# Scratch stores and loads of a two-layer hybrid backbone, issued from GpSimd and ScalarE instead of SyncE

## The chip, the cores and the metric

The kernel runs on one core of a Trainium2 chip. The metric is the device time of one execution in microseconds; the median of three runs is given with the lowest and the highest. The profile is of one execution, and times inside it count from the start of its span. Engines are named as in the profile: PE is TensorE (its weight loads are PEld), DVE is VectorE, ACT is ScalarE, POOL is GpSimd, SP is SyncE. A name with a q behind it (SPq, POOLq) is the engine's instruction queue, where DMAs are issued and waits stand.

## The reference

Two layers work on 512 latent and 256 context tokens of width 1024 in float32. Each layer normalises and modulates its tokens and multiplies them with one wide input matrix. Its columns feed four mixers: A, attention over all tokens with normalised queries and keys and a rotary step; B, a gating unit that mixes positions inside blocks of 128; C, attention in a window of 128 tokens with a sink; D, an mLSTM that scans six blocks in both directions. What joins them is this:

```python
def merge_branches(ys, p, w_br, w_o):
    gates = (p['a_gate'], p['w_gate'], p['g_gate'], p['m_gate'])
    y = jnp.stack([yk * jax.nn.silu(gk) for yk, gk in zip(ys, gates)], axis=2)
    proj = jnp.einsum('bnkw,kwd->bnkd', y, w_br)
    m = p['merge']
    g = jax.nn.sigmoid(m.reshape(m.shape[0], m.shape[1], N_BRANCH, D_MODEL))
    return jnp.sum(g * proj, axis=2) @ w_o
```

The result is normalised, gated and added to the tokens. In the second layer the outputs of context tokens are not needed.

## The kernel before

Tokens lie in tiles of 128: latent tiles 0 to 3 and context tiles 4 and 5. Each matrix product is made of three passes with the high and low parts of both factors, in a 32-bit format that PE takes (fp32r). A weight block goes through `emit_load` (L210): two DMAs into staging buffers `wr` (three of them, L222), ScalarE makes the high part `wh` (L224), VectorE the low part `wl` (L225); there are two buffers of each.

A layer has two stages. In the **mixer stage** two threads are interleaved at the time the program is built (`interleave`, L1219). The dense thread multiplies the tokens with column blocks of the input matrix, in an order chosen from `FILL_ORDER` (L71), and each block has its own ending: gates (`gate_unit`, L545), the sigmoids of the merge that are computed early (`early_unit`, L559), the mLSTM's output gate (`mo_unit`, L573) and its convolved q, k and v (`m_unit`, L586). Until they are needed these results lie in **scratch tensors** in device memory: `sgd`, `thd`, `omd`, `zd`. The mixer thread runs attention A, the mLSTM's gate arithmetic (`gate_math`, L854), window attention, and the four heads of the mLSTM (`mlstm_prep`, L947, and `mlstm_scan`, L1007). It reads the mLSTM's inputs back (L957, L1019), reads rows of `nmd` spread over all partitions (L987; ScalarE's L991 is the first to use them) and stores the branches' outputs to `ydram` (L837, L1068) and the softmax sums to `rsd` (L831). The gating unit (`spatial`, L619) runs in the merge stage of layer 0 and in the mixer stage of layer 1; it stores through `turn_out` (L673).

In the **merge stage** (`merge`, L1266) the four branches follow each other. For each of four column tiles the branch's output `yt` and gate `sg` are read back (L1279, L1280), for the two attentions also the inverted sums `rs`, each row spread over 64 partitions (two DMAs, L1284). VectorE multiplies them (L1286, L1287), ScalarE and VectorE split the product into `gh` and `gl` (L1288, L1289), and PE multiplies those with the branch's projection for eight column tiles; an early sigmoid `th` is read back for each (L1300). `yt`, `sg`, `rs` and `th` come from one pool of eight buffers `m`. `finish` (L1357) makes the output projection, normalises and adds; in layer 0 it stores the new tokens (L1412) and prepares the next layer's input.

`rstd` (L352) computes a power of -1/2 on GpSimd (L354): 72 small instructions, GpSimd's only work besides four fills at the start.

Every DMA but two at the start (ScalarE, L152 and L163) is issued from the SyncE queue, in order. The framework orders each engine's instructions by priority in a simulated time line and adds the waits; the order on hardware is then fixed, engine by engine. An instruction whose data or buffer is not ready holds everything behind it on its engine.

Of the kernel before, what the change touches and what calls it, by code (L numbers as in the profile page):

```python
# [83 lines left out]
def tile_hybrid_block(ctx, tc, A, out):  # L84
# [61 lines left out]
    # constants  # L146
# [131 lines left out]
    def side(units):  # L278
        """Units of later uses, their rows of weights summed up by VectorE, in small steps."""
        def load(l, i, half):  # L280
            raw = wp.tile([128, UW // 2], F32, tag="wr", name="wr", bufs=3)[:, :1024]
            sy.dma_start(out=raw, in_=A["w_mod"][l, i][:, half * 1024:half * 1024 + 1024])
            return v3(raw, 4)

        sums = None
        for l, i in units:
            ns = 2 if l == 0 or i < 8 else 1
            for half in range(2):
                raw = load(l, i, half)
                yield  # L290
                if half == 0:
                    if sums is not None:
                        side_sums(*sums)
                    acc = [T1() for _ in range(ns)]
                    sums = (l, i, acc)
                for k in range(4):
                    kk = 4 * half + k
                    for s in range(ns):
                        if kk == 0:
                            dve.tensor_scalar(acc[s], raw[:, k, :], cH[:, kk, s:s + 1], None, op0=ALU.mult)  # L300
                        else:
                            dve.scalar_tensor_tensor(out=acc[s], in0=raw[:, k, :], scalar=cH[:, kk, s:s + 1],
                                                     in1=acc[s], op0=ALU.mult, op1=ALU.add)
                    if k % SIDE_K == SIDE_K - 1 and k < 3:
                        yield
        yield
        side_sums(*sums)
# [36 lines left out]
    def load_gates(l, i):  # L344
        if i % 2 == 0:
            g = gate_g[l, i // 2] = M(512)
            sy.dma_start(out=g, in_=bc(gates[l][0:1, i * 256:i * 256 + 512], [128, 512]))
        if l == 0:
            gate_c[i] = XS()
            sy.dma_start(out=gate_c[i], in_=bc(gates[l][1:2, i * 256:i * 256 + 256], [128, 256]))  # L350
# [73 lines left out]
    def seg_mm(wh, wl, mh, ml, nk, seg):  # L424
        """One column tile over one token segment."""
        ps = DB()
        n = seg.stop - seg.start
        for k in range(nk):
            mm(ps[:, :n], wh(k), mh(k)[:, seg], k == 0, False)
            mm(ps[:, :n], wh(k), ml(k)[:, seg], False, False)  # L430
            mm(ps[:, :n], wl(k), mh(k)[:, seg], False, k == nk - 1)
        return ps[:, :n]
# [16 lines left out]
    def rope_tables(g):  # L449
        """cos and sin rows times a norm's weights; sin by its source half."""  # L450
        tab = M(512).rearrange("p (s t d) -> p s t d", s=2, t=XT)
        gv = bc(g.rearrange("p (o d) -> p o d", o=1), [128, XT, 64])
        dve.tensor_mul(tab[:, 0], cosT, gv)
        dve.tensor_mul(tab[:, 1], sinT, gv)
        return tab[:, 0], tab[:, 1]

    def evacuate(ps, nh, g):
        """First stage of a tile of heads: out of PSUM, with the norm's factors."""
        n = nh * 64
        e, a = T1()[:, :n], T1()[:, :n]  # L460
        act.copy(e, ps[:, :n])
        r = None
        if g is not None:
            act.activation(a, ps[:, :n], AF.Square)
            ss = YD(4)[:, :nh]
            dve.tensor_reduce(out=ss, in_=a.rearrange("p (h d) -> p h d", h=nh), op=ALU.add, axis=AX.X)
            r = rstd(YD(4)[:, :nh], ss, nh, 64.0, EPS)
        return e, a, r

    def rotate(ear, nh, t, g, tabs, copies):  # L470
        """Second stage: norm, rotary and the split into copies of high and low parts."""
        e, a, r = ear
        shape = [128, nh, 64]
        ev, av = (z.rearrange("p (h d) -> p h d", h=nh) for z in (e, a))
        if r is not None:
            dve.tensor_mul(ev, ev, bc(r.rearrange("p (h o) -> p h o", o=1), shape))
        if t < XT:
            dve.tensor_mul(av, ev, bc(tabs[0][:, t:t + 1, :], shape))
            dve.tensor_mul(ev, ev, bc(tabs[1][:, t:t + 1, :], shape))
            dve.tensor_add(av[:, :, 0:32], av[:, :, 0:32], ev[:, :, 32:64])  # L480
            dve.tensor_add(av[:, :, 32:64], av[:, :, 32:64], ev[:, :, 0:32])
            ev, e = av, a
        elif g is not None:
            dve.tensor_mul(ev, ev, bc(g.rearrange("p (o d) -> p o d", o=1), shape))
        st = ST()
        sv = st.rearrange("p (h s d) -> p h s d", h=nh, s=2 * copies)
        f = e.rearrange("p (h o d) -> p h o d", h=nh, o=1).to_broadcast([128, nh, copies, 64])
        act.copy(sv[:, :, 0:copies, :].bitcast(F32R), f)
        dve.tensor_sub(sv[:, :, copies:, :].bitcast(F32R), f, sv[:, :, 0:copies, :])
        return st  # L490
# [11 lines left out]
    def drain(n2, n3):  # L502
        """Runs the waiting stages of earlier tiles, all but the last n2 and n3."""
# [41 lines left out]
    def gate_unit(l, b, i, sgd, segs):  # L545
        w = in_unit(l, f"gate{b}_{i}")
        for c in range(2):
            for seg in segs:
# [7 lines left out]
                sy.dma_start(out=sgd[b, 2 * i + c][:, seg], in_=th[:, :n])  # L556
                yield seg_us(seg)

    def early_unit(l, name, thd, segs):  # L559
        b, i = int(name[1]), int(name[3])  # L560
        wh, wl = take(("in", l, name))
        for c in range(2):
            mh, ml = (v3(w[:, c * 1024:c * 1024 + 1024], 8) for w in (wh, wl))
            for seg in segs:
# [5 lines left out]
                sy.dma_start(out=thd[b, 2 * i + c][:, seg], in_=th[:, :n])  # L570
                yield seg_us(seg)

    def mo_unit(l, i, omd, nq):  # L573
# [3 lines left out]
        for t in range(nq):  # L577
# [5 lines left out]
            sy.dma_start(out=omd[2 * i:2 * i + 2, :, t * 128:(t + 1) * 128].rearrange("h p d -> p h d"), in_=v3(th, 2))  # L583
            yield TOK_US

    def m_unit(l, i, zd, res):  # L586
        taps = res["taps"]
        w = in_unit(l, f"m{i}")
        for c in range(2):
# [3 lines left out]
            for seg in segs:  # L593
# [11 lines left out]
                sy.dma_start(out=zd[j][:, seg], in_=zz)  # L605
# [4 lines left out]
    def gelu2(dst, ps, acc=None):  # L610
        """dst = 2 gelu(ps), and its sum over the columns"""
# [61 lines left out]
    def turn_out(v, dst):  # L673
# [5 lines left out]
        sy.dma_start(out=dst.rearrange("g p t -> p g t"), in_=v3(ys, 2))  # L679
# [22 lines left out]
    def attend_scores(qT, kv, kT, hl, pair, mode, sc, sink, sums):  # L702
        is_x = pair[0] < XT
        Ps = []
        for t in pair:
            ps = S()
            qs = qT[:, hl, t * 128:(t + 1) * 128]
            # pieces: (psum column, key column, count)
# [44 lines left out]
    def attend_values(Ps, Vt, kv, pair, mode, yT, hl):  # L753
        is_x = pair[0] < XT
        # blocks: (key tile, first query, number of queries)
# [41 lines left out]
    def attention(l, mode, b, ydram, rsd, res):  # L797
# [26 lines left out]
        # the queries' sums, inverted and as rows, to divide by where the branch is read back  # L824
# [6 lines left out]
        sy.dma_start(out=rsd[b].rearrange("h (t q) -> (h t) q", q=128), in_=rows[:8 * nq, :])  # L831

    def finish_attend(pend, ydram, b, mode):
        Ps, Vt, kv, pair, yT, hl, hp = pend
        yield from attend_values(Ps, Vt, kv, pair, mode, yT, hl)
        if hl % 2 == 1:
            sy.dma_start(out=ydram[b, 2 * kv + hp][:, pair[0] * 128:pair[0] * 128 + 256], in_=yT)  # L837

# [15 lines left out]
    def gate_math(l, G):  # L854
        """All decay quantities, laid out as (direction, chunk, head) columns."""
# [63 lines left out]
        # floor: 2 exp(-(b + max(m_prev, cummax u)))  # L919
# [16 lines left out]
        # rows of -M_t  # L936
# [6 lines left out]
        sy.dma_start(out=nmd, in_=oth)  # L943
# [3 lines left out]
    def mlstm_prep(h, gm, zd, nq, res):  # L947
# [7 lines left out]
        for r, z in enumerate((qT, kT, vT)):  # L955
            n = nq * 128 if r == 0 else NTOK
            sy.dma_start(out=z[:, :n], in_=zd[3 * h + r][:, :n])  # L957
        # token-layout k and v
# [12 lines left out]
        # S^T, shared by the directions  # L971
# [12 lines left out]
        for d in range(2):  # L984
            rows = gm["nmd"][d * 32 + h:d * 32 + h + 24:4, :][:nq]
            nm, qs, kw = B2[:, 2 * d, :], B2[:, 2 * d + 1, :], (vT, kT)[d]
            sy.dma_start(out=v3(nm[:, :n], nq),  # L987
# [19 lines left out]
    def mlstm_scan(l, h, gm, pre, omd, nq, ydram):  # L1007
# [4 lines left out]
        for s in range(NT):  # L1012
# [4 lines left out]
            if s == NT - 2:  # L1017
                om = M(768)
                sy.dma_start(out=om[:, :n], in_=omd[h][:, :n])  # L1019
# [32 lines left out]
        # per-head norm, output gate, transposition  # L1052
# [15 lines left out]
        sy.dma_start(out=ydram[3, h][:, :n], in_=H[:, :n])  # L1068
        yield 0.7

# [54 lines left out]
    def needs(name):  # L1125
        """Buffers of the two pools that a unit takes."""
        return int(name[:2] == "w_" or name == "g_v0"), int(name in ("w_kv", "g_v0"))

    def pick(left, cur, res):
        """The first unit left that needs not wait once the current one has its buffers."""  # L1130
# [74 lines left out]
    def fits(res, c):  # L1205
        """Whether a mark is set, or a pool has so many free buffers."""
# [12 lines left out]
    def interleave(X, Dn, res, ratio):  # L1219
        """Emits the mixers' steps and the dense steps in proportion; each may wait for marks of the other."""  # L1220
# [4 lines left out]
        def dstep():  # L1225
            """Cost of one dense step, or None when it has to wait or has ended."""
# [39 lines left out]
    def merge(l, ydram, rsd, sgd, thd):  # L1266
# [8 lines left out]
        for bi, b in enumerate(BRANCHES):  # L1275
            gh, gl = BIG([128, 4, NTOK], F32R), BIG([128, 4, NTOK], F32R)
            for k in range(4):
                yt, sg = M(768), M(768)
                sy.dma_start(out=yt[:, :n], in_=ydram[b, k][:, :n])  # L1279
                sy.dma_start(out=sg[:, :n], in_=sgd[b, k][:, :n])  # L1280
                if b < 2:
                    rs = M(768)
                    for i in range(2):
                        sy.dma_start(out=rs[64 * i:64 * i + 64, :n],  # L1284
# [5 lines left out]
            for j in range(KT):  # L1290
# [5 lines left out]
                if (l, b, j // 2) in EARLY:  # L1296
# [3 lines left out]
                    sy.dma_start(out=th[:, :n], in_=thd[b, j][:, :n])  # L1300
# [92 lines left out]
    def finish_tile(l, t, o, sst, xdram):  # L1393
# [17 lines left out]
        if t < XT:  # L1411
            sy.dma_start(out=xdram[t], in_=o)  # L1412
# [11 lines left out]
    def next_x(t, xn):  # L1424
        """Normalised and modulated input of the next layer, transposed and split."""
# [48 lines left out]
def _layout(I):  # L1474
# [46 lines left out]
    # shape constants  # L1521
# [39 lines left out]
```

## Time and profile before

| | |
|---|---|
| Runs, us | 2069.32, 2072.67, 2073.26; median 2072.67 |
| Profiled execution, span, us | 2072.0 |
| PE busy | 2006.9 us (97%), 13196 matmuls |
| PEld, DVE, ACT, POOL busy | 88%, 64%, 47%, 3% |
| DMA | 274.97 MB, mean 133 GB/s, q1 40.5% of the 16 engines' time |

The profiled execution is known by its span; the page gives no other time for it. PE's busy time is nearly the whole span in every slice but the first and the last ones. A busy PE means that matmuls are under way; they overlap, so it does not say how close to its peak PE is. A row of waits tells who stood idle, for whom, how long in all, how often, and the longest single wait. Waits of an engine that is not the bottleneck cost nothing by themselves.

### The profile page before, as it was taken

The page shows a single profiled execution, that of the slowest core. Times are in us where ns is not written, and L with a number is a line of the kernel's source. Part 1 is how long each engine was busy: PE and PEld are TensorE (multiplying, and loading weights), DVE is VectorE, ACT ScalarE, POOL GpSimd, SP SyncE. Part 2 cuts the span into 40 slices and gives each one's busy share as a digit, 9 for nine tenths or more (in the row PEclk, how much of TensorE's full clock was granted, in tenths as well). Part 3 has the DMA queues.
Part 4 walks back from the last instruction along what each step waited for, and adds up shares of the span by engine and source line. Part 5 has one row for each costly group of instructions (what it writes and reads, how often), then busy time and mean ns, then how long its engine had stood idle before and what let it go on. Part 6 is the DMA issues. An engine that isn't in the chain of part 4 may idle for free. (4 is left out here: it accounts for less than half of the span.)

```text
span 2072.0 us, 34558 instructions
## 1 busy us (share of the span) xinstructions
PE 2006.9 (97%) x13196; PEld 1816.9 (88%) x13196; DVE 1321.5 (64%) x2861; ACT 978.5 (47%) x2195; POOL 69.0 (3%) x76
## 2 busy tenths in 40 slices
PE   7999999999999999999999999999999999999998
PEld 4998998999999898889998999989989898887777
DVE  5766766676556665648545588667676575555765
ACT  6565554344444444324432376655554465433333
POOL 0200100000000000001000022000000000000000
PEclk9999999999999999999999999999999999999999
DMA  7212223323333534665334352223334325447745
GB/s 279 73 44 85 81 86 115 123 98 112 122 117 96 172 122 149 198 206 184 114 116 140 123 190 67 86 96 112 92 121 139 123 90 161 147 147 224 246 136 178
DMA packets 133142, 274.97 MB, mean 133 GB/s; under 512 B 16176, under 2 KB 52208, under 8 KB 132592
## 3 DMA queue, kind: packets, MB, share of 16 engines
q1 hardware_dynamic: 132688, 272.69, 40.5%
q8 instruction: 104, 1.70, 0.3%
q14 instruction: 62, 0.51, 0.1%
q10 hardware_dynamic: 288, 0.07, 0.0%
HBM read 219.33 MB, written 53.37 MB: 132 GB/s over the span
## 5 line engine op out<-in xcount | busy, mean ns | idle before, releaser
L238 PE MATMUL d<-xh,wh 128*128 128x512 f32 (+1 forms) x1504 | 538.0, 358 | 0.1
L238 PE MATMUL d<-xh,wl 128*128 128x512 f32 (+1 forms) x1504 | 535.9, 356 | 0.0
L238 PE MATMUL d<-xl,wh 128*128 128x512 f32 (+1 forms) x1504 | 535.2, 356 | 0.0
L225 DVE TENSOR_TENSOR wl<-wr,wh 128x1024 fp32r<-128x1024 f32 (+3 forms) x274 | 294.5, 1096 | 67.9 <-ACT wh L224 64.8
L224 ACT CAST wh<-wr 128x1024 fp32r<-128x1024 f32 (+3 forms) x274 | 248.8, 950 | 182.5 <-PE s L238 81.7
L238 PEld LDWEIGHTS d<-xh,wh 128*128 128x128 f32 x1504 | 285.6, 190 | 35.0 <-DVE st L604 0.3
L238 PEld LDWEIGHTS d<-xh,wl 128*128 128x128 f32 x1504 | 285.4, 190 | 34.4
L238 PEld LDWEIGHTS d<-xl,wh 128*128 128x128 f32 x1504 | 285.6, 190 | 33.7
L238 PE MATMUL d<-wh,xh 128*128 128x256 f32 (+1 forms) x992 | 287.1, 290 | 5.6 <-ACT t L614 1.4
L238 PE MATMUL d<-wl,xh 128*128 128x256 f32 (+1 forms) x992 | 283.3, 286 | 0.3 <-DVE wl L225 0.3
L238 PE MATMUL d<-wh,xl 128*128 128x256 f32 (+1 forms) x992 | 282.5, 286 | 0.6 <-DVE xl L401 0.4
L238 PEld LDWEIGHTS d<-wh,xh 128*128 128x128 f32 x992 | 189.8, 192 | 7.2 <-ACT t L614 1.6
L238 PE MATMUL s<-big,wh 128*128 128x512 f32 x720 | 184.1, 362 | 9.6 <-DVE big L1289 8.0
L238 PEld LDWEIGHTS d<-wh,xl 128*128 128x128 f32 x992 | 190.0, 192 | 1.3 <-DVE xl L401 0.8
L238 PEld LDWEIGHTS d<-wl,xh 128*128 128x128 f32 x992 | 190.3, 192 | 0.9 <-DVE wl L225 0.5
L780 DVE TENSOR_TENSOR m<-s,m 128x768 fp32r<-128x768 f32 (+2 forms) x144 | 119.4, 836 | 95.2 <-ACT m L779 94.6
L744 ACT ACTIVATE m<-s,yx 128x768 f32<-128x768 f32 (+3 forms) x160 | 120.2, 752 | 92.8 <-DVE yx L742 46.0
L238 PEld LDWEIGHTS s<-big,wh 128*128 128x128 f32 x720 | 120.4, 191 | 32.8 <-DVE big L1289 9.2
L738 DVE TENSOR_REDUCE yx<-s 128x1 f32<-128x768 f32 (+3 forms) x160 | 122.5, 765 | 34.9 <-PE s L238 33.8
L779 ACT CAST m<-s 128x768 fp32r<-128x768 f32 (+2 forms) x144 | 100.8, 704 | 88.6 <-PE s L776 88.0
L238 PE MATMUL b<-m,v 128*128 128x256 f32 (+1 forms) x768 | 132.3, 286 | 4.0 <-ACT m L779 4.0
L238 PE MATMUL s<-big 128*128 128x256 f32 (+2 forms) x680 | 119.7, 304 | 1.3 <-ACT big L496 0.7
(289 smaller groups left out, 3035.0 us busy)
## 6 DMA issues: line engine op xcount, KB each, us to landing
wr<-in_w_in_dram SPq DMA_DIRECT2D x100, 512.0 KB, 4.2
wr<-in_w_mg_dram SPq DMA_DIRECT2D x50, 512.0 KB, 4.3
wr<-in_w_mod_dram SPq DMA_DIRECT2D x42, 512.0 KB, 5.3
wr<-in_w_out_dram SPq DMA_DIRECT2D x32, 512.0 KB, 3.7
th<-st SPq DMA_DIRECT2D x50, 256.0 KB, 4.7
wr<-in_w_bp_dram SPq DMA_DIRECT2D x50, 256.0 KB, 3.9
wr<-in_w_br_dram SPq DMA_DIRECT2D x28, 384.0 KB, 4.2
m<-th SPq DMA_DIRECT2D x26, 384.0 KB, 6.0
```

The costliest lines, as they stand in the source:

```text
L224: act.copy(wh[:, sl], raw[:, :hn])
L225: dve.tensor_sub(wl[:, sl], raw[:, :hn], rd(wh[:, sl]))
L238: pe.matmul(o, l, r, start=start, stop=stop)
L738: dve.reduce_max(out=mx, in_=ps[:, :n], axis=AX.X)
L744: act.activation(P, ps[:, :n], AF.Exp, bias=nm[:, 0:1], scale=sc, accum_out=sm)
L779: act.copy(ph, pt[:, :n])
L780: dve.tensor_sub(pl, pt[:, :n], rd(ph))
```

## The change

No computation changes. The loads of `load_gates`, all scratch loads, the stores of what VectorE made, a few stores of ScalarE's copies (L831, L1068) and the store of the new tokens go to GpSimd's queue (`pool.dma_start`). Two stores whose data ScalarE has just made go to ScalarE's queue (`act.dma_start`): those of `early_unit` and of `turn_out`. Weights, constants, the tokens read in `finish_tile` (L1405) and the output (L1408) stay on SyncE. Comments and docstrings fall away too, without moving a line. The lines that matter:

```diff
@@ load_gates
-            sy.dma_start(out=g, in_=bc(gates[l][0:1, i * 256:i * 256 + 512], [128, 512]))
+            pool.dma_start(out=g, in_=bc(gates[l][0:1, i * 256:i * 256 + 512], [128, 512]))
...
-            sy.dma_start(out=gate_c[i], in_=bc(gates[l][1:2, i * 256:i * 256 + 256], [128, 256]))
+            pool.dma_start(out=gate_c[i], in_=bc(gates[l][1:2, i * 256:i * 256 + 256], [128, 256]))
@@ gate_unit
-                sy.dma_start(out=sgd[b, 2 * i + c][:, seg], in_=th[:, :n])
+                pool.dma_start(out=sgd[b, 2 * i + c][:, seg], in_=th[:, :n])
@@ early_unit
-                sy.dma_start(out=thd[b, 2 * i + c][:, seg], in_=th[:, :n])
+                act.dma_start(out=thd[b, 2 * i + c][:, seg], in_=th[:, :n])
@@ mo_unit
-            sy.dma_start(out=omd[2 * i:2 * i + 2, :, t * 128:(t + 1) * 128].rearrange("h p d -> p h d"), in_=v3(th, 2))
+            pool.dma_start(out=omd[2 * i:2 * i + 2, :, t * 128:(t + 1) * 128].rearrange("h p d -> p h d"), in_=v3(th, 2))
@@ m_unit
-                sy.dma_start(out=zd[j][:, seg], in_=zz)
+                pool.dma_start(out=zd[j][:, seg], in_=zz)
@@ turn_out
-        sy.dma_start(out=dst.rearrange("g p t -> p g t"), in_=v3(ys, 2))
+        act.dma_start(out=dst.rearrange("g p t -> p g t"), in_=v3(ys, 2))
@@ attention
-        sy.dma_start(out=rsd[b].rearrange("h (t q) -> (h t) q", q=128), in_=rows[:8 * nq, :])
+        pool.dma_start(out=rsd[b].rearrange("h (t q) -> (h t) q", q=128), in_=rows[:8 * nq, :])
@@ finish_attend
-            sy.dma_start(out=ydram[b, 2 * kv + hp][:, pair[0] * 128:pair[0] * 128 + 256], in_=yT)
+            pool.dma_start(out=ydram[b, 2 * kv + hp][:, pair[0] * 128:pair[0] * 128 + 256], in_=yT)
@@ gate_math
-        sy.dma_start(out=nmd, in_=oth)
+        pool.dma_start(out=nmd, in_=oth)
@@ mlstm_prep
-            sy.dma_start(out=z[:, :n], in_=zd[3 * h + r][:, :n])
+            pool.dma_start(out=z[:, :n], in_=zd[3 * h + r][:, :n])
...
-            sy.dma_start(out=v3(nm[:, :n], nq),
+            pool.dma_start(out=v3(nm[:, :n], nq),
@@ mlstm_scan
-                sy.dma_start(out=om[:, :n], in_=omd[h][:, :n])
+                pool.dma_start(out=om[:, :n], in_=omd[h][:, :n])
...
-        sy.dma_start(out=ydram[3, h][:, :n], in_=H[:, :n])
+        pool.dma_start(out=ydram[3, h][:, :n], in_=H[:, :n])
@@ merge
-                sy.dma_start(out=yt[:, :n], in_=ydram[b, k][:, :n])
-                sy.dma_start(out=sg[:, :n], in_=sgd[b, k][:, :n])
+                pool.dma_start(out=yt[:, :n], in_=ydram[b, k][:, :n])
+                pool.dma_start(out=sg[:, :n], in_=sgd[b, k][:, :n])
...
-                        sy.dma_start(out=rs[64 * i:64 * i + 64, :n],
+                        pool.dma_start(out=rs[64 * i:64 * i + 64, :n],
...
-                    sy.dma_start(out=th[:, :n], in_=thd[b, j][:, :n])
+                    pool.dma_start(out=th[:, :n], in_=thd[b, j][:, :n])
@@ finish_tile
-            sy.dma_start(out=xdram[t], in_=o)
+            pool.dma_start(out=xdram[t], in_=o)
```

## Rows read from the trace of the kernel before

**Rows 1.** The page: busy time by engine, and the DMA queue q1.

```profile
PE 2006.9 (97%) x13196; PEld 1816.9 (88%) x13196; DVE 1321.5 (64%) x2861; ACT 978.5 (47%) x2195; POOL 69.0 (3%) x76
...
q1 hardware_dynamic: 132688, 272.69, 40.5%
```

**Rows 2.** Windows: us, busy PE, PEld, DVE, ACT, POOL (instructions), granted clock, DMA share, GB/s.

```profile
0.00:66.00 66.00, 50.51 (x301) 35.22 (x302) 41.67 (x89) 38.13 (x84) 5.54 (x13) 0.90 0.69 243
700.00:720.00 20.00, 16.96 (x102) 15.04 (x101) 12.45 (x34) 11.85 (x30) 0.00 (x0) 0.91 0.50 169
780.00:795.00 15.00, 11.63 (x74) 10.80 (x73) 7.15 (x23) 8.84 (x21) 0.00 (x0) 0.89 0.48 153
865.00:890.00 25.00, 19.24 (x104) 15.96 (x103) 14.58 (x38) 7.46 (x25) 1.32 (x1) 0.80 0.88 266
1085.00:1105.00 20.00, 17.16 (x90) 14.73 (x89) 13.52 (x17) 4.88 (x8) 0.00 (x0) 0.91 0.69 237
1935.00:1975.00 40.00, 34.39 (x140) 26.92 (x139) 32.24 (x52) 12.27 (x20) 0.00 (x0) 0.96 0.75 235
```

**Rows 3.** PE's longest wait in those five stretches, in order: total, times, longest.

```profile
PE b L238 <- ACT m L779: 3.0, 1, 3.0
...
PE b L238 <- DVE xs L1030: 3.4, 1, 3.4
...
PE d L238 <- ACT big L1288: 5.6, 2, 3.6
...
PE s L238 <- DVE big L1289: 2.8, 1, 2.8
...
PE s L238 <- DVE big L1289: 5.2, 2, 2.6
```

**Rows 4.** ACT's waits for the mLSTM rows: whole span, then 700 to 720.

```profile
ACT big L991 <- DMA big<-nmd: 23.9, 10, 7.6
...
ACT big L991 <- DMA big<-nmd: 4.2, 2, 3.0
```

**Rows 5.** Timeline of ACT, 777 to 787: start, us, instruction [idle before <-releaser].

```profile
786.16 0.98 ACT L991 ACTIVATE big<-big,gmp 128x128 f32<-128x128 f32 x3 [7.63 <-DMA big<-nmd]
```

**Rows 6.** Waits of the SyncE queue, the longest in total.

```profile
SPq L222 <- DVE wl L225: 523.3, 155, 27.7
```

**Rows 7.** DMA issues by tile, first and last group moved: count, KB, landing us.

```profile
m<-th SPq DMA_DIRECT2D x26, 384.0 KB, 6.0
...
rs<-xs SPq DMA_DIRECT2D x2, 16.0 KB
```

**Rows 8.** Lines L570, L987 and L1284: issue ns min/median/max; landing of L987 and L1284.

```profile
L570 SPq DMA_DIRECT2D th<-st x76: 319/326/1871, 340.6 to 1872.9; - x76
...
L987 SPq DMA_DIRECT2D big<-nmd x16: 359/438/545, 556.2 to 1801.0; - x16
...
DMA to landing us min/median/max: 3.8/3.8/3.8
...
DMA to landing us min/median/max: 3.3/4.1/5.4
```

**Rows 9.** Timeline of ACT at the start: its own DMA.

```profile
1.17 0.46 ACTq L163 DMA_DIRECT2D st<-in_c_ident_dram  x1
```

**Rows 10.** Line L354, the powers on POOL: ns min/median/max.

```profile
L354 POOL TENSOR_TENSOR yd<-yd,mhalf x64: 548/958/2218, 13.6 to 2066.8; 128x1 f32<-128x1 f32 x32, 128x4 f32<-128x4 f32 x20, 128x2 f32<-128x2 f32 x12
```

**Rows 11.** Waits of DVE over the span.

```profile
DVE m L1286 <- DMA m<-rs: 36.9, 13, 5.9
...
DVE m L1287 <- DMA m<-sg: 24.2, 10, 8.6
...
DVE yx L356 <- POOL yx L354: 6.2, 5, 1.4
```

**Rows 12.** Timeline of the SyncE queue, 775 to 780.

```profile
776.61 0.42 SPq L222 DMA_DIRECT2D wr<-in_w_mg_dram  x1
778.32 0.97 SPq L987 DMA_DIRECT2D big<-nmd  x2
```

## The prediction

> **What bounds the kernel now.** I read the page's busy table first, then the granted clock by stretch, PE's waits, and the queues. PE is busy for 2006.9 of 2072.0 us, 97% [rows 1], so at most 65.1 us can be won. The first 66 us, in which no scratch is moved, hold 15.5 of them (66.00 less 50.51) [rows 2]; 49.6 are left. PE's waits show which of these end with scratch data. There are five stretches: 3.0 us at 700 to 720 and 3.4 us at 780 to 795 [rows 3], while ScalarE stands in front of the mLSTM rows (L991, `big<-nmd`) for 4.2 us [rows 4] and 7.6 us [rows 5]; 5.6 us at 865 to 890, 2.8 us at 1085 to 1105 and 5.2 us at 1935 to 1975, where a branch's factors (L1288, L1289) are late for its projection [rows 3]. That is 20.0 us. In each of these stretches the granted clock is under 1 [rows 2]: a part ran at 1.2 GHz instead of 2.4. They lost 20 x 0.09 + 15 x 0.11 + 25 x 0.20 + 20 x 0.09 + 40 x 0.04 = 11.9 us to that. Together **31.9 us, 1.5% of the span, is all that faster scratch traffic can give**. The rest of PE's time is matmuls that follow each other.
>
> The SyncE queue is in order and holds weights and scratch alike. It stands for 523.3 us in front of weight loads whose staging buffer VectorE has not released [rows 6]. Waiting of a queue costs only what it makes late. The five stretches hold no PE wait for a weight; scratch behind the weights is what can be late.
>
> **The change, part by part.** Counted by tile in the DMA issue view, 468 DMAs leave SP: 96 for ScalarE (76 `th` stores, 20 stores of L679) and 372 for GpSimd, 170 stores and 202 loads, in 32 groups from `m<-th` x26 to `rs<-xs` x2 [rows 7]. No bytes are added. SP loses 468 issues of about 0.33 us [rows 8]; PE doesn't wait for SP's time, so I cost that at nothing. Its cover is the staging buffer: a weight load can't go before VectorE releases it, whatever left the queue.
>
> *ScalarE's 96 issues.* Its own DMA at the start took 0.46 us [rows 9]. 96 x 0.46 = 44 us are added to 978.5 us of work [rows 1], spread over both layers. In the five stretches PE waits 3.0 + 5.6 = 8.6 us for ScalarE [rows 3]; 44/978.5 of that is 0.4 us. With the smaller waits elsewhere I take **+1 us**, bounds 0 and +5. ScalarE's idle half hides the rest; a store waits only for the activation just before it.
>
> *GpSimd's price per DMA.* The trace of before has no DMA on POOL. From below the nearest row is SP's issue, 0.33 us [rows 8]; from above POOL's longest instruction, 2.2 us. I take POOL's median instruction, about 1.0 us [rows 10], the row nearest to what this engine needs for any instruction. So an issue takes 0.6 us longer than on SP, and 0.5 us longer for the broadcasts, which took SP some 0.44 us [rows 8]. 372 x 1.0 us is a fifth of the span: POOL has room, only chains feel it.
>
> *mLSTM rows (L987, 16 loads in 8 pairs).* The second of a pair is 2 x 0.5 = 1.0 us later, and ScalarE takes both in order: 8 us. By L985 to L988 such a load has 768 pieces of 512 B in layer 0, where an ordinary tile has 128 rows. If making pieces is slower on POOL, that shows here most: from 0 to a doubled landing, 3.8 us [rows 8], each; I take 1 us, near the lower end, since SP's issue of these is only 0.1 us longer: 16 us. Of ScalarE's 4.2 + 7.6 us, 3.0 + 3.4 reached PE, 0.54 [rows 3 to 5]. So 24 x 0.54 = **+13 us**, bounds 0 and (8 x 3.5 + 61) x 0.54 = +48.
>
> *Branch factors (L1279 to L1284).* In the first two branches a pair of `rs` broadcasts stands between a freed buffer and VectorE's product; it waited for `rs` 13 times, 36.9 us, and for `sg` 10 times, 24.2 us [rows 11]. 13 x 1.0 and 10 x 0.6 us later make 19 us on VectorE. The three merge stretches cost PE 13.6 us [rows 3] against these 61.1, 0.22: **+4 us**. Bounds 0 and, at 2.2 us an issue, (13 x 3.5 + 10 x 1.9) x 0.22 = +14.
>
> *Less queueing behind weights.* Nearly all traffic is on one queue, q1 [rows 1]. At 776.61 a weight load of 512 KB, the second of two in a row, went out ahead of the pair of row loads at 778.32 [rows 12]; ScalarE began at 786.16 [rows 5], 6.9 us after the pair's issue, against 3.8 us for the one such landing on record [rows 8]. With the rows in another ring those 3 us come back, and 1.6 us of clock: -4.6. In the merge stretches weights stand between the loads too. An `rs` landing spreads from 3.3 to 5.4 us around 4.1 [rows 8], so each of their five stalls gets 1 us: -5. At 700 to 720 I find only scratch in the way (`z`), which moves along: 0. Sum **-10 us**, bounds 0 and -31.9.
>
> The Trainium skill, page "DMA: Bandwidth & Descriptors", section "Issuing engines are not separate DMA queues", speaks against this gain: DMAs of all issuers run on the same 16 engines, and several issuers only save issue time. By it this term is 0 and the sum +19 us, 2092 us; the trace of before, with one busy queue, can't show it.
>
> *The powers.* POOL also computes every `rstd` (L354), 64 times here [rows 10] and 8 in the mLSTM; VectorE's longest total wait for it is 6.2 us, at L356 [rows 11]. With POOL a fifth busy issuing, a power meets one under way in 0.18 of cases and waits half of it: 72 x 0.18 x 0.5 = 6.5 us on VectorE, 0.22 of which is **+1 us**; bounds 0 and the in-order rival. At the layer boundary the store of L1412 comes before a power, but a square (L1414) and L353 lie between: nothing, and without that cover four stores of 1.0 us.
>
> Sum: 1 + 13 + 4 - 10 + 1 = +9 us on the profiled 2072.0 us. The median of the runs, 2072.67, lies 0.7 us above that span, so **2082 us**, +0.4%.
>
> **The rivals.**
> *Separate queues win.* POOL issues as cheaply as SP (0.33 us) and scratch no longer lies behind weights or their buffers. The plus terms shrink to 5 us and the five stretches lose two thirds, -21: -16 us, 2057 us; at the most -31.9, 2041. For it: 7.6 us of waiting with weights ahead [rows 5, 12] and 523.3 us of blocking [rows 6]. Against: a scratch load has to wait for a buffer of its own as well. Chance 0.30.
> *It cancels.* POOL at 0.65 us: the plus terms halve and -10 stands: 2072 us. Chance 0.17.
> *POOL in order becomes the wait.* A load that waits for its buffer holds the powers behind it, and VectorE, in order too, stands at L1060 or L690. SP's waits of this sort are 523.3/155 = 3.4 us [rows 6], 3 us taken; for the 18 powers of the mLSTM and the gating unit that is 54 us on VectorE, a third of which reaches PE: +18. With half the upper bound of the row loads, +24: +42 us, 2115 us. It decides once POOL's median DMA takes over 2 us or L356 and L690 wait 3 us for POOL. Against: powers are few. Chance 0.14.
> The Trainium skill, page "SBUF — State Buffer", section "SBUF: two separate sides", names a way to it: GpSimd can't write a DMA's descriptors while VectorE runs a 2-port operation. No row here shows it.
> *It isn't carried out as written*: POOL's DMAs go through q1 as before. Only the order changes, 2073 us. Chance 0.03.
>
> **How the numbers follow.** The forecast has 0.36, its own range 2077 to 2097. Runs of this kernel tell about 0.2%, 4 us, from no change. Faster is the first rival, 0.30; same is cancelling and not carried out, 0.20; slower is the forecast and the in-order rival, 0.50. The range from 2046 to 2115 leaves out the far end of the first rival (0.07) and half of the in-order one (0.07), and holds the bounds of POOL's price.
>
> **What would show it.** POOL gets 372 DMAs; a median near 1.0 us bears out the price. L991's waits for `big<-nmd` rise from 23.9 us [rows 4] to some 45 if the rows are slower to make, and fall below 10 if separate queues win. L1286's waits for `rs` pass 45 us. A second large queue stands beside q1. I am wrong if PE's idle time after 66 us falls below 40 us, or if POOL's DMAs take under 0.5 us.

## The result and the profile after

| | before | after |
|---|---|---|
| Runs, us (7 each, on one chip) | 2062.82 to 2073.26, median 2069.32 | 2073.00 to 2085.09, median 2079.05 |
| Profiled execution, us | span 2072.0 | 2084.19, span 2082.4 |

The ratio is **1.0054, 95% interval 1.0038 to 1.007**: slower by about half a per cent, 11 us. The page of the changed kernel, set against [rows 1], gives the busy time and then the DMA queues (packets, MB, share):

```profile
PE 2011.3 (97%) x13196; PEld 1818.4 (87%) x13196; DVE 1323.9 (64%) x2861; ACT 979.5 (47%) x2195; POOL 279.2 (13%) x448
...
q1 hardware_dynamic: 54512, 160.31, 23.9%
q0 software_dynamic: 25760, 93.23, 14.4%
q10 hardware_dynamic: 16672, 19.22, 2.6%
```

GpSimd has 448 - 76 = 372 instructions more and 279.2 - 69.0 = 210.2 us more of work, 0.57 us for one DMA. Its DMAs have a queue of their own, q0, and ScalarE's have q10. PE does the same work, 4.4 us slower, at a granted clock of 0.987 over the span instead of 0.988. Single executions of the kernel before lie between 0.986 and 0.993, so this part may be chance. The other 6.0 us of the 10.4 between the two spans are idle time. Of the first 66 us PE was idle for 14.8 (window below), so behind them it was idle for 71.1 - 14.8 = 56.3 us, where before it was 49.6.

```profile
0.00:66.00 66.00, 51.17 (x316) 34.72 (x317) 42.34 (x92) 38.87 (x86) 5.54 (x13) 0.95 0.70 243
```

These are the waits of the changed kernel (total, times, longest) over the span, to be set against [rows 4, 6, 11]:

```profile
ACT big L991 <- DMA big<-nmd: 33.0, 12, 6.3
...
DVE m L1286 <- DMA m<-rs: 23.4, 11, 4.3
DVE m L1287 <- DMA m<-sg: 15.4, 7, 5.7
DVE yx L356 <- POOL yx L354: 4.1, 3, 1.5
...
PE d L238 <- ACT big L1288: 8.6, 4, 4.7
PE s L238 <- DVE big L1289: 5.8, 5, 2.7
...
SPq L222 <- DVE wl L225: 1163.0, 164, 35.5
```

The two rows of PE, for which [rows 3] has only windows, were these over the span of the kernel before:

```profile
PE s L238 <- DVE big L1289: 8.0, 3, 2.8
...
PE d L238 <- ACT big L1288: 6.1, 3, 3.6
```

Three things are to be seen. The wait for the mLSTM rows grew from 23.9 to 33.0 us. VectorE's waits for `rs` and `sg` did not grow but fell, and PE's two waits for the branch factors hardly moved, 14.4 us against 14.1. And SyncE now waits 1163.0 us instead of 523.3 for a staging buffer: relieved of the scratch, it stands at the next weight load and sends it the moment VectorE lets the buffer go.

The lines of the DMAs themselves, L987, L1284 and, as an ordinary tile, L1279 (issue ns min/median/max, then landing us), are to be set against [rows 8]:

```profile
L987 POOL DMA_DIRECT2D big<-nmd x16: 759/799/852, 561.6 to 1823.6; - x16
...
DMA to landing us min/median/max: 3.7/6.4/10.2
```

```profile
L1284 POOL DMA_DIRECT2D m<-rs x32: 527/534/576, 857.9 to 1926.3; - x32
...
DMA to landing us min/median/max: 2.8/4.2/7.0
```

```profile
L1279 POOL DMA_DIRECT2D m<-yd x32: 536/548/582, 839.0 to 1974.9; - x32
```

One more thing lies between the two kernels that no line of the diff says. The framework orders instructions by a simulated time line, and with other queues it made **another order**: compared by line and tile in the two traces, ScalarE's sequence first differs at 158 us and those of VectorE and PE at some 230 us, and some 1600 of PE's 13196 matmuls stand in another place. So the two traces differ by the queues and by the order at once, and a wait that is shorter or longer after the change may be due to either.

### The profile page after: what moved, and what is told of

Read it like the earlier page. It is cut to its first block, busy times and chain, and to the rows that moved or that the text cites. A ratio compares the mean times of both kernels' runs of the same rounds, so it can differ in the third digit from the quotient of the medians.

```text
span 2082.4 us, 34627 instructions
## 1 busy us (share of the span) xinstructions
PE 2011.3 (97%) x13196; PEld 1818.4 (87%) x13196; DVE 1323.9 (64%) x2861; ACT 979.5 (47%) x2195; POOL 279.2 (13%) x448
## 3 DMA queue, kind: packets, MB, share of 16 engines
q1 hardware_dynamic: 54512, 160.31, 23.9%
q0 software_dynamic: 25760, 93.23, 14.4%
## 5 line engine op out<-in xcount | busy, mean ns | idle before, releaser
L780 DVE TENSOR_TENSOR m<-s,m 128x768 fp32r<-128x768 f32 (+2 forms) x144 | 120.0, 837 | 103.3 <-ACT m L779 102.5
```

Source lines behind the costliest of these rows:

```text
L780: dve.tensor_sub(pl, pt[:, :n], rd(ph))
```

## Experiments

To part the two I added to a kernel a list of all instructions in one kernel's order, and tied each engine's neighbours in that list by an ordering that adds no semaphore (shortened here: `listed_order` is unpacked from a coded list, and `NO_SYNC` stands for the framework's name of such a dependency):

```diff
+    for i in listed_order:
+        ins = traced[i]
+        if ins.engine in last:
+            tc.add_manual_dep(ins, last[ins.engine], NO_SYNC, reason="order")
+        last[ins.engine] = ins.name
```

Both kernels have the same instructions, so either's queues can be run in either's order. In every run with a list PE, VectorE and ScalarE keep the sequence of the kernel that the table names. GpSimd, which had no DMA before, takes its powers and DMAs in the sequence that the list gives them together. All results, in us and as a ratio to the kernel before on the same chip, from 4 to 12 executions of each run:

| run | moved off SyncE | order of | median | ratio | 95% interval |
|---|---|---|---|---|---|
| p_ab | all 468 | before | 2103.81 | 1.0176 | 1.0161 to 1.0192 |
| p_ba | none | after | 2072.70 | 1.0019 | 1.0008 to 1.003 |
| p_nm | all but L987 | before | 2083.68 | 1.0079 | 1.0061 to 1.0098 |
| p_act | ScalarE's 96 stores | before | 2067.36 | 1.0001 | 0.9989 to 1.0014 |
| p_rows | L987 alone | before | 2070.61 | 1.0016 | 1.0002 to 1.003 |
| p_ld | the 202 loads | before | 2083.50 | 1.0080 | 1.0058 to 1.0102 |
| p_st | the 266 stores | before | 2073.98 | 1.0029 | 1.0015 to 1.0043 |
| t1 | all but L987 | framework's own | 2075.31 | 1.0032 | 1.0018 to 1.0046 |
| p_h | all but L1068 | before | 2096.29 | 1.0135 | 1.0108 to 1.0161 |
| p_vs | all but L556, L583, L605 | before | 2093.00 | 1.0120 | 1.0096 to 1.0144 |
| p_free | all 468 | before, GpSimd's left free | 2095.39 | 1.0129 | 1.0105 to 1.0153 |
| p_an | all but L987 | after | 2080.29 | 1.0059 | 1.0045 to 1.0073 |

### Queues and order apart

**p_ab**: the changed kernel's queues with the list of before.

> All 468 DMAs move as in the change, but every engine keeps the order of instructions that it has in the kernel before (the framework's simulated time line made another order of PE, VectorE and ScalarE for the changed kernel). Price theory (the prediction's: GpSimd's price on the chains for the mLSTM rows and the branch factors is the cost): +9 us, ratio about 1.004, with ScalarE's waits for the rows at L991 above the 23.9 us of before. Order theory (the other order of the instructions is the cost, the queues themselves are worth little): 0.998 to 1.001, PE's idle time back near that of before.

**p_ba**: the kernel before with the list of after.

> All DMAs stay on SyncE as before, but every engine has the order of instructions of the changed kernel. Price theory: nothing slower is issued, so 0.999 to 1.001. Order theory: the loss is here without any DMA moved, 1.004 to 1.007, in the mixer stages and not in the merges.

Neither theory holds. The new order alone, with the queues of before, costs 0.19%, 4 us. The queues alone, in the order of before, cost 1.76%, **36 us**, four times the sum of the prediction; with the order that the framework makes for them, 1.0054, some 25 us of that are gone. In that order the queues cost 1.0054 - 1.0019 = 0.35%, 7 us. The framework's list was a repair, not the cost. In the profiled executions (p_ab's is the longest of its four) the span of p_ab is 34.3 us longer than that of before: PE is idle for 92.3 us instead of 65.1, and its busy time is 7.1 us longer, at a granted clock of 0.983 instead of 0.988.

Part of the 7 us that the queues cost in the new order is seen by comparing p_ba with the changed kernel, same order and other queues. PE's waits in p_ba for the branches' factors:

```profile
PE d L238 <- ACT big L1288: 6.7, 4, 5.0
...
PE s L238 <- DVE big L1289: 2.7, 4, 1.8
```

They total 9.4 us against 14.4 in the changed kernel: 5 us in the merges. All listed waits of PE together differ by as much, 58.5 us against 63.4, but not only there: a wait of 8.7 us at L961 in p_ba is gone in the changed kernel (below), and smaller ones have come. So the 7 us are shown as a sum, not wait by wait.

**p_act**: two stores of the change alone, with the list of before.

```diff
@@ early_unit
-                sy.dma_start(out=thd[b, 2 * i + c][:, seg], in_=th[:, :n])
+                act.dma_start(out=thd[b, 2 * i + c][:, seg], in_=th[:, :n])
@@ turn_out
-        sy.dma_start(out=dst.rearrange("g p t -> p g t"), in_=v3(ys, 2))
+        act.dma_start(out=dst.rearrange("g p t -> p g t"), in_=v3(ys, 2))
```

> Only the 96 stores of ScalarE's data (L570, L679) move, to ScalarE's queue; everything else and the order of instructions as before. Price theory: +1 us (0 to 5), ratio 1.000 to 1.002. Order theory: 1.000 as well; a ratio above 1.002 would say that ScalarE's issues are worth more than either gave them.

1.0001: ScalarE's issues and the list together can't be told from nothing.

### Rows, loads and stores

**p_nm** is p_ab with one line put back:

```diff
-            pool.dma_start(out=v3(nm[:, :n], nq),
+            sy.dma_start(out=v3(nm[:, :n], nq),
```

> As the first run (all queues of the change, order of before), but the 16 loads of the mLSTM rows (L987) stay on SyncE. Price theory: these 16 loads were the largest plus term, +13 us, less some 5 us for queueing behind weights, so this is about 8 us (0.4%) faster than the first run. Order theory: same as the first run within 0.1%.

**p_rows** is the opposite edit: only this line goes to GpSimd.

> Only the 16 loads of the mLSTM rows (L987) move to GpSimd, order of before. Putting these loads back gave 20.1 us of the 35.9 us of the first run (2103.81 less 2083.68). Price theory (making 768 pieces and the longer landing on GpSimd is the cost, whoever else uses the queue): +13 to +20 us, ratio 1.006 to 1.010. Company theory (the loads are late because GpSimd's queue, in order, stands in front of stores and powers whose data is not ready): without stores in that queue at most +5 us, under 1.0025.

With everything else on GpSimd the 16 row loads are worth 1.76 - 0.79 = 0.97%, 20 us; alone they cost 0.16%, 3 us. A price that belongs to the load would be the same in both. The line of L987 in p_rows (issue, who waits, landing):

```profile
L987 POOL DMA_DIRECT2D big<-nmd x16: 747/814/996, 550.7 to 1799.2; - x16
...
  ACT big L991: 24.9, 11
...
DMA to landing us min/median/max: 4.1/6.4/9.3
```

The issue takes 0.8 us and the landing up to 9.3, as in the changed kernel, yet ScalarE waits 24.9 us, 1.0 more than before [rows 4]. Landing that late was nothing new. From SyncE too, rows issued at 778.32 were used at 786.16 [rows 5, 12], and p_ba, with the rows on SyncE, has these landings of L987; the 3.8 us of [rows 8] were one landing, and an early one:

```profile
DMA to landing us min/median/max: 4.7/6.2/6.9
```

In company ScalarE's wait is longer; in p_ab and then in p_nm:

```profile
ACT big L991 <- DMA big<-nmd: 38.1, 11, 12.1
```

```profile
ACT big L991 <- DMA big<-nmd: 27.5, 12, 11.0
```

**p_ld** moves L347, L350, L957, L987, L1019, L1279, L1280, L1284 and L1300 to GpSimd and leaves the stores; **p_st** moves the ten lines of stores and leaves the loads.

> All 202 scratch loads move to GpSimd, the 266 stores stay on SyncE, order of before. Price theory: nearly the whole 1.0176 of the first run, 1.014 to 1.018, as stores carry no price. Company theory: about a third of it, 1.003 to 1.008, the rest being stores that hold loads.

> All 266 scratch stores move as in the change (170 to GpSimd, 96 to ScalarE), the 202 loads stay on SyncE, order of before. Price theory: 0.998 to 1.001, as no load waits for a store's issue. Completion theory (the rows of the second and fourth head reuse the buffer that the store of L1068 reads, and that store lands later from GpSimd than the 2.6 us it took from SyncE): 1.002 to 1.005, with the issue of the rows at L987 in the first layer's last pair late behind that store. Separate-queue theory (loads and weights no longer stand behind stores that wait for data): below 0.997.

Loads alone cost 0.80%, at the upper end of the company theory; stores alone 0.29%, inside the completion theory. Together they cost 1.76%, so 0.67%, 14 us (by the intervals 0.4 to 1.0%), is there only when both are moved. Price theory falls, and the separate-queue theory most clearly: **no run in a kept order gains anything from taking scratch off the weights' queue**.

### What the company does

In p_ab the longest wait of ScalarE for the rows, 12.1 us, stands before 794.47. This is the timeline of p_ab around it: GpSimd, SyncE's queue, ScalarE (start, us, instruction, idle before and releaser).

```profile
780.07 0.61 POOL L1068 DMA_DIRECT2D yd<-big  x1 [10.63 <-ACT big L1067]
788.35 1.65 POOL L987 DMA_DIRECT2D big<-nmd  x2 [7.67 <-PE d L238]
...
779.11 0.33 SPq L222 DMA_DIRECT2D wr<-in_w_in_dram  x1
780.25 0.33 SPq L222 DMA_DIRECT2D wr<-in_w_mg_dram  x1
...
778.99 0.78 ACT L1067 COPY big<-s 128x768 f32<-128x768 f32 x1
794.47 1.86 ACT L991 ACTIVATE big<-big,gmp 128x128 f32<-128x128 f32 x6 [12.11 <-DMA big<-nmd]
```

The rows are written into a buffer of the tag `big`. In the kernel before, the same three DMAs stood so (SyncE's queue; the loads and rows are [rows 12]):

```profile
775.70 0.32 SPq L1068 DMA_DIRECT2D yd<-big  x1
776.11 0.41 SPq L222 DMA_DIRECT2D wr<-in_w_in_dram  x1
```

The line of L1068 gives the landing of that one store, us min/median/max, before and then in p_ab:

```profile
DMA to landing us min/median/max: 2.6/2.6/2.6
```

```profile
DMA to landing us min/median/max: 7.8/7.8/7.8
```

Before, the rows went out 2.6 us after the store, when it had landed. In p_ab they went out 8.3 us after it, when it had landed there. The row of 788.35 names a matmul of the dense thread, which neither reads nor writes `big`; but GpSimd's own wait in front of these rows (ns, start) is as long as the landing:

```profile
L987 POOLq EVENT_SEMAPHORE  x1: 7804/7804/7804, 780.1 to 780.1; - x1
```

So the rows wait until the store of the finished head has left `big`. On one queue that store was ahead of the two 512 KB weight loads; on a queue of its own it is not: the first weight load goes out 0.96 us earlier than the store, as soon as its staging buffer is free, the second 0.18 us behind it. **p_h** undoes this one line in p_ab:

```diff
-        pool.dma_start(out=ydram[3, h][:, :n], in_=H[:, :n])
+        sy.dma_start(out=ydram[3, h][:, :n], in_=H[:, :n])
```

> The first run (all queues of the change, order of before, 1.0176) with the 8 stores of the mLSTM heads (L1068) kept on SyncE. Completion theory: the rows of the second head pair no longer wait for a store that took 7.8 us from GpSimd against 2.6 us from SyncE; 8 to 14 us come back, ratio 1.011 to 1.014. In-order theory (loads stand behind stores that wait for VectorE's data, whichever they are): 8 of 266 stores change little, 1.016 to 1.018.

The ratio falls by 0.41%, 8.5 us, for 8 stores of 468 DMAs; the two intervals touch at 1.0161, so the size is known to some 6 us either way. The same place in p_h, SyncE and then GpSimd:

```profile
779.42 0.33 SPq L1068 DMA_DIRECT2D yd<-big  x1
779.84 0.41 SPq L222 DMA_DIRECT2D wr<-in_w_in_dram  x1
780.34 0.42 SPq L222 DMA_DIRECT2D wr<-in_w_mg_dram  x1
...
782.58 1.69 POOL L987 DMA_DIRECT2D big<-nmd  x2 [13.81 <-ACT big L962]
```

The store is ahead of the weights again, and the rows follow it after 3.2 us instead of 8.3. They start right behind ScalarE's L962, which ends at 782.46, so the store had landed by then.

That GpSimd's issue alone doesn't make the landing late is seen in the changed kernel. There the store is on GpSimd too, but in the new order the last weight load before it goes out 8 us earlier, and the rows follow it after 3.2 us as well (SyncE, then GpSimd):

```profile
773.58 0.33 SPq L222 DMA_DIRECT2D wr<-in_w_mg_dram  x1
...
781.84 0.62 POOL L1068 DMA_DIRECT2D yd<-big  x1 [10.21 <-ACT big L1067]
785.07 1.66 POOL L987 DMA_DIRECT2D big<-nmd  x2 [2.62 <-PE s L961]
```

**p_vs** asks for the other half: loads standing in GpSimd's queue behind stores that wait for VectorE. GpSimd's waits in p_ab:

```profile
POOL yd L354 <- DVE yd L353: 269.9, 46, 44.8
POOL sg L556 <- DVE st L554: 228.7, 30, 26.4
POOL yd L837 <- DVE xs L794: 180.0, 18, 37.9
POOL z L605 <- DVE st L604: 176.5, 31, 20.9
```

The edit puts L556, L583 and L605 back on SyncE.

> The first run (1.0176) with the 112 stores of VectorE's data that GpSimd waits longest for (L556, L583, L605: 228.7, 68.4 and 176.5 us for their first releaser) put back on SyncE. In-order theory: the loads behind them go out in time, 1.008 to 1.011, near the 1.008 of loads alone. Completion theory (only the store of L1068 matters): 1.016 to 1.018.

1.0120: 0.56%, 11.6 us, come back, a little short of what the in-order theory asked. ScalarE's wait at L991 falls from 38.1 to 32.2 us with it. That the loads had been held in the queue by these stores fits the result, but the trace doesn't show it load by load.

The store's landing and the stores ahead of the loads both cost time. How p_nm's 20 us, p_h's 8.5 and p_vs's 11.6 share the 36 of p_ab stays open: each is uncertain by 5 to 6 us, and p_nm still has a wait of 11.0 us at the place that p_h mends.

**p_free** leaves GpSimd's own order to the framework.

> The first run (1.0176) with PE, VectorE, ScalarE and SyncE in the order of before, but GpSimd's own order left to the framework. If what the framework's order repaired in the changed kernel (1.0054) lies in GpSimd's queue, this is 1.005 to 1.010. If it lies in when PE, VectorE and ScalarE do the work around the late loads, 1.015 to 1.018.

1.0129, between the two: some 10 of the 25 us lie in GpSimd's queue, the rest in what PE, VectorE and ScalarE do meanwhile. Only about ten of GpSimd's 448 instructions stand in another place than in p_ab, among them three stores of L1068 that go out earlier. So some 10 of p_ab's 36 us belong to the sequence that the list gave to GpSimd, not to the queues as such.

### The rows in the change as it runs

**t1** is the changed kernel with L987 on SyncE, in the order that the framework makes for that; **p_an** is the same with the list of after.

> The change itself, in the order that the framework makes for it, with the 16 loads of L987 put back on SyncE. Price theory: the rows are the largest term of the change as it runs, so 0.998 to 1.001, at least 8 us below the changed kernel. If the framework's order has already covered the rows' delay: 1.004 to 1.006, as the changed kernel.

> The changed kernel with its own order of instructions kept as it is, and the 16 loads of L987 back on SyncE. With that order the queues of before gave 1.0019 (p_ba) and those of the change 1.0054, so the queues cost 0.35%, some 7 us. If the rows are the main part of that (the prediction's largest term, +13 before -4.6 for queueing): at most 1.003. If the branch factors and the rest carry it: 1.0045 or more. If the order takes up the rows' delay wholly: 1.005 to 1.006.

t1 is 0.22% below the change, 4.5 us, but its interval and the change's overlap. p_an is at 1.0059, not below it at all. ScalarE's wait for the rows is no measure of the time here: in t1 it is 35.3 us, more than in the change. In p_an's trace ScalarE's wait at L991 falls from 33.0 to 28.5 us, but PE has a wait that it does not have in the changed kernel and has, at 8.7 us, in p_ba:

```profile
PE s L961 <- DVE m L780: 8.1, 1, 8.1
```

So in that order the rows are worth nothing: all listed waits of PE total 63.4 us with the rows on either queue, and what goes elsewhere comes back at L961. The traces show where that wait comes from. PE waits for VectorE's L780, and VectorE stands just before it at L805, in front of the small load of `sink` (L804, SyncE). SyncE and VectorE in p_an:

```profile
707.18 0.96 SPq L987 DMA_DIRECT2D big<-nmd  x2
709.15 0.34 SPq L804 DMA_DIRECT2D sink<-in_w_sink_dram  x1
...
721.02 0.17 DVE L805 TENSOR_SCALAR sink<-sink 128x8 f32<-128x8 f32 x1 [11.22 <-DMA sink<-in_w_sink_dram]
```

The same in the changed kernel, whose GpSimd sends the rows at 710.91:

```profile
710.47 0.33 SPq L804 DMA_DIRECT2D sink<-in_w_sink_dram  x1
...
712.98 0.17 DVE L805 TENSOR_SCALAR sink<-sink 128x8 f32<-128x8 f32 x1 [1.85 <-DMA sink<-in_w_sink_dram]
```

Behind the rows `sink` is used 11.9 us after its issue, ahead of them 2.5 us after. A queue of its own isn't what saves it: in p_ld the rows go out on GpSimd 5.7 us ahead of it, and it is used 10.9 us after its issue. No run moves L804 alone.

## Why the prediction was right in sum and wrong in its terms

The forecast of +9 us stands beside 1.0054, 11 us. That the two agree is luck, since the runs show a sum of other things: +36 us for the queues in the order that the prediction reasoned in, and -25 us by a new order, of which it did not think (+27 and -15 with GpSimd's sequence left to the framework, p_free).

- **ScalarE's issues, +1.** Held: 1.0001 in p_act, an issue 0.33 us instead of the 0.46 taken.
- **GpSimd's price, 1.0 us.** Mis-sized: 0.55 us for an ordinary tile, 0.80 for the rows (the lines of the changed kernel above), 210.2/372 = 0.57 on the mean; inside the bounds and nearer to SyncE's 0.33. What GpSimd needs for a power said little of what it needs for a DMA.
- **mLSTM rows, +13.** The step that failed is a fixed price per load times the share that reaches PE. The runs show 3 us alone, 20 in company in the order of before, and none to 4.5 in the change as it runs. Nor do the rows land later from GpSimd than from SyncE: 6.4 us at the median in p_rows, 6.2 in p_ba. The forecast of some 45 us of waiting at L991 was 33.0, and 38.1 in p_ab.
- **Branch factors, +4.** Half held. In one order the size is right: PE's two waits are 5 us longer in the change than in p_ba. Between the two kernels themselves they differ by 0.3 us, since the new order had made them shorter, 9.4 us in p_ba against 14.1. The sign that I named did not come: L1286's waits for `rs` were to pass 45 us and are 23.4. In the order of before they do reach 44.1 (p_ab); the other order has 22.6 of them even with all on SyncE (p_ba).
- **Less queueing behind weights, -10.** This failed. I read the rows' 6.9 us, against 3.8 for the one landing on record, as the price of the weight load ahead of them. From a queue of their own the rows land no sooner, 6.4 us at the median (p_rows and the change), so there was nothing to give back; and what kept them until 778.32 was the landing of the store at 775.70, not the weight load. The term also counted its gains in full, where the plus terms counted only the share that reaches PE, 0.54 or 0.22. No run gains by isolation, and p_ab against p_h shows the reverse: on its own queue the scratch loses its place ahead of the weights. The Trainium skill, page "DMA: Bandwidth & Descriptors", section "Issuing engines are not separate DMA queues", says that transfers of all issuers interleave on the same engines; the trace agrees, with a store that took 7.8 us to land beside the weights, where it had taken 2.6 ahead of them. By that rule the term was 0 and the sum +19 us, which lies between the change's 11 and p_ab's 36.
- **The powers, +1, SyncE's relief, 0, and the layer boundary, 0.** VectorE's wait at L356 is 4.1 us, and 4.0 in p_ba, so the powers cost nothing in the change; in the order of before it goes from 6.2 to 7.7 us (p_ab). SyncE's relief only became waiting, 1163.0 us at L222. The boundary was not tried by itself.
- **The rivals.** Separate queues do not win. Of GpSimd in order I had the wrong half: I priced powers held by loads. VectorE hardly waits for powers; it is the loads that go out late, and p_vs puts 11.6 us on three lines of stores that wait for VectorE. GpSimd's powers wait for VectorE too, 269.9 us in p_ab, but no run parts them from the loads behind them. "Its median DMA takes over 2 us" was not the point from which that decides.

Still open is which moves in the framework's order win back the 15 us that are not in GpSimd's queue, and which waits make up the 7 us that the queues cost in that order. None of the twelve runs beats the kernel before: p_act equals it.

## What to carry to other kernels

Where a framework orders the instructions, moving a DMA to another queue changes the order too: compare the two orders first, and pin one, before a wait is put down to the queue. A shared in-order queue is also a priority: a small store whose landing frees the next buffer keeps its place ahead of bulk loads only while it shares their queue. The traces of p_an and of the change show the same of a small load, late when it is issued behind the spread rows and early when ahead of them. Move loads and stores in separate runs; here both together cost 14 us more than the two added up.

## What the runs showed of the hardware

GpSimd sends the spread rows in larger packets than SyncE. The page's packet line of p_nm, with the rows on SyncE, and then of p_ab:

```profile
DMA packets 106071, 274.97 MB, mean 132 GB/s; under 512 B 16177, under 2 KB 36625, under 8 KB 105521
```

```profile
DMA packets 97110, 274.97 MB, mean 131 GB/s; under 512 B 16176, under 2 KB 26384, under 8 KB 96560
```

The packets under 2 KB differ by 10241, and the 16 loads have 8 x 768 + 8 x 512 = 10240 pieces of 512 B by L985 to L988. From GpSimd these pieces are gone from the small packets. p_rows has nothing but the 16 loads in GpSimd's queue, 1536 packets of 3.4 KB on the mean:

```profile
q0 software_dynamic: 1536, 5.24, 1.5%
```

They did not land sooner for it: 6.4 us at the median and up to 9.3 in p_rows, against 6.2 and 6.9 from SyncE in p_ba. I had expected the making of 768 pieces to be what GpSimd is slow at; the issue took 0.80 us, against 0.55 for an ordinary tile.
